# Two networks in one kernel: low halves, dots and one-hots placed anew

## The chip, the cores and the metric

The kernel runs on one core of a Trainium2 chip, in one launch. The metric is the device time in microseconds; a kernel's time is the median of its runs. The engines are named as the profile names them: PE is TensorE, DVE is VectorE, ACT is ScalarE, POOL is GpSimd, SP is SyncE (here only a queue that starts loads).

## The reference

The input is 256 tokens of width 1024, and two networks of two layers each follow one another. The first has three mixers and a feed-forward of inner width 2816: `x + (silu(h @ w_gate) * (h @ w_up)) @ w_down`. The second has attention over the tokens and a context of 256 more tokens, and a feed-forward made of experts, which is where most of the time goes:

```python
s1 = einsum('nhd,kd->nhk', q1, sub_keys[0]); s2 = einsum('nhd,kd->nhk', q2, sub_keys[1])
v1, i1 = top_k(s1, 16); v2, i2 = top_k(s2, 16)
top_s, pos = top_k(v1[..., :, None] + v2[..., None, :], 16)     # 16 of 16384 experts, 8 heads
expert = take_along_axis(i1 * 128 + i2, pos)
u = u_tab[expert]
act = gelu(einsum('nhkd,nd->nhk', u, hb))
out = einsum('nhk,nhkd->nd', softmax(top_s) * act, v_tab[expert])
```

Each of 256 tokens picks 128 of 16384 experts (rows of 1024 numbers in two tables, U and V), in each of two layers. In layer 0 the 256 context tokens pass through the experts too.

## The kernel before

Products need more than one pass of TensorE's fp32r format: an operand is split into a high half (`hi`, a copy by ACT) and a low half (`lo = x - hi`, a subtract), and a product is three matmuls, hi*hi, hi*lo and lo*hi. `Net.split` (lines 172 to 181) does this with ACT and, for `lo`, DVE or POOL.

**Experts for the main tokens, dense (`Dense`).** All 16384 experts are computed for all 256 tokens, as 128 groups of 128 experts, cut into parts: four of 32 groups in layer 0, two of 64 in layer 1. Three kinds of steps exist. A U step (`u_part`) loads 512 KB of U, splits it and makes 24 matmuls, then a gelu into the tile A. A one-hot step (`w_part`, called W here; 32 per part, 8 tokens each) builds on DVE a one-hot of the first index (`o1`), one of the second (`o2`), and two products with the gate (`og`); 16 matmuls turn these into the weights of the part's experts, and DVE multiplies A by them. A V step (`v_part`) loads 512 KB of V, splits it and a column of A (`w_hi`, `w_lo`) and makes 12 matmuls that add to the output. `mesh` interleaves such steps at a fixed ratio. The order in layer 0 before is: U0 (beside the routing); U1 with W0; V0 with W1; U2; V1 with W2; U3; V2 with W3; V3. In layer 1 it is U0; U1 with W0; V0 with W1; V1. The subtract of U goes to POOL and DVE by columns (`self.low`: POOL has 2 of 8 column blocks in parts 0 and 1 of layer 0, else 4 of 8), that of V half to each. Raw tiles, split tiles and one-hots have a few buffers each (3 and 1 more for raw tiles in layer 0), and the next load waits until the splits have read a raw tile.

**Experts for the context tokens, gathered (`peer_gather`).** POOL starts an indirect DMA for each of 256 U rows (128 tokens' row each, 512 KB) and 256 V rows. For a U row a dot with the token's vector follows: either POOL multiplies and ACT sums, or DVE does both in one instruction. The first block's first 60 rows (`EARLY`) use POOL, and of the rows from 118 on every third (`POOL_DOTS`). V rows go to TensorE in fours. These rows are started during the first network's layer 1, and run on through its feed-forward, the attention and the expert block of layer 0.

**The order of work.** The engines execute their queues in order. A scheduler puts the instructions into the queues by priority and by a simulated time; `rank` and `issue_after` set priorities of the gather and of the attention, which are issued among other work.

**The second feed-forward** (`First.ffn`, called for layer 1 in the scope `f1`) makes 22 blocks of `act` in one loop; a second loop loads `w_down` in 22 pieces, splits each (every fourth on POOL), splits `act` (its low half on POOL) and multiplies.

Of the kernel before, what the change touches and what calls it, by code (L numbers as in the profile page):

```python
# [297 lines left out]
class First:  # L298
# [209 lines left out]

    def ffn(self, l, x, after=None, more=None):

        nc, n, a = self.nc, self.n, self.a
        hT, _ = self.norm_T(x, self.vcol("ffn_norm_g", l, 8), "hT2")
        if after:
            after()
        act = self.zones["x"].tile([P, KF, S], F32, name="ffact")
        for c in range(KF):
            ps = self.psum("pgu")
            for i, name in enumerate(("ffn_w_gate", "ffn_w_up")):
                w = self.w.load(a[name][l, c], KD, P, "wgu")
                for k in range(KD):  # L520
                    n.mm3(ps[:, i * S : (i + 1) * S], part(w, k), part(hT, k), k == 0, k == KD - 1)
            th = self.t([P, S], "ffth")
            nc.scalar.activation(th, ps[:, :S], AF.Tanh, scale=0.5)
            nc.vector.tensor_scalar(th, th, 0.5, 0.5, op0=ALU.mult, op1=ALU.add)
            nc.vector.tensor_tensor(th, ps[:, :S], th, op=ALU.mult)
            nc.vector.tensor_tensor(act[:, c], ps[:, S:], th, op=ALU.mult)
        wd = a["ffn_w_down"][l].rearrange("(k p) c -> p k c", p=P)
        pss = [self.psum(f"pd{i}") for i in range(4)]
        for k in range(KF):
            ws = self.w if more is None or k % 2 else more  # L530
            if k % 4 < 2:
                w = part(ws.load(wd[:, k : k + 1], 1, D, "wd"), 0)
            else:
                if k % 2 == 0:
                    two = self.zones["x"].pair([P, 2, D], "wd2")
                w = part(two, k % 2)
                raw = ws.plain(wd[:, k : k + 1], 1, D, "wd")
                n.split(raw[:, 0], *w, eng2="gv"[k % 2])
            ak = self.z.pair([P, S], "ffak")
            n.split(act[:, k], *ak, eng2="g")  # L540
            for b in range(2):
                for hf in range(2):
                    n.mm3(pss[2 * b + hf], part(ak, slice(b * P, (b + 1) * P)), part(w, slice(hf * 512, (hf + 1) * 512)), k == 0, k == KF - 1)
        for b in range(2):
            for hf in range(2):
                xs = x[:, b, hf * 512 : (hf + 1) * 512]
                nc.vector.tensor_tensor(xs, pss[2 * b + hf], xs, op=ALU.add)
# [438 lines left out]
class Second:  # L986
# [408 lines left out]
    def peer_gather(self, slots, rows, out, gp, vp, act0, hm0):  # L1395
# [11 lines left out]
        def u_rows(b):  # L1407
# [4 lines left out]
            def dot(j, u):  # L1412
                o = act[:, j : j + 1]
                if j < EARLY if b == 0 and j < EARLY + GATHERS else j % POOL_DOTS == 0:
                    nc.gpsimd.tensor_tensor(u, u, hm, op=ALU.mult)  # L1415
                    nc.scalar.activation(u, u, AF.Copy, accum_out=o)
                else:
                    nc.vector.tensor_tensor_reduce(out=u, in0=u, in1=hm, scale=1.0, scalar=0.0, op0=ALU.mult, op1=ALU.add, accum_out=o)  # L1418
# [84 lines left out]
class Dense:  # L1503
# [9 lines left out]
    def __init__(self, net, ctx, x, h, l, col, parts, banks, raw):  # L1513
# [5 lines left out]
        self.parts = parts  # L1519
        self.low = ((2, 2, 4, 4), (4, 4))[l]  # L1520
        self.first = [sum(parts[:i]) for i in range(len(parts))]
# [32 lines left out]
    def u_part(self, f, A):  # L1554
# [3 lines left out]
        def split(i):  # L1558
# [3 lines left out]
            ul = self.pu.tile([P, KD, P], F32R, tag="lo", name="u_lo")  # L1562
            q = self.low[f]
            nc.scalar.activation(uh, u, AF.Copy)  # L1564
            for e, o, m in ((nc.gpsimd, 0, q), (nc.vector, q, KD)):
                if o < m:
                    e.tensor_tensor(ul[:, o:m], u[:, o:m], uh[:, o:m].bitcast(F32), op=ALU.subtract)  # L1567
            return uh, ul
# [69 lines left out]
    def v_part(self, f, W, starts, stops):  # L1638
# [4 lines left out]
        for i in range(H):  # L1643
# [4 lines left out]
            vl = self.pu.tile([P, D], F32R, tag="lo", name="v_lo")  # L1648
            nc.scalar.activation(vh, v, AF.Copy)  # L1649
            nc.gpsimd.tensor_tensor(vl[:, 0:512], v[:, 0:512], vh[:, 0:512].bitcast(F32), op=ALU.subtract)  # L1650
            nc.vector.tensor_tensor(vl[:, 512:], v[:, 512:], vh[:, 512:].bitcast(F32), op=ALU.subtract)  # L1651
            wh = self.po.tile([P, S], F32R, tag="wh", name="w_hi")
# [55 lines left out]
LOW = "gv"  # L1708
POOL_DOTS = 3
GATHER_CLASSES = ((32, 8), (512, 5), (1024, 2), (4096, 1))  # L1710
# [7 lines left out]
def build(tc, aps, out):  # L1718
    with ExitStack() as ctx:
# [99 lines left out]

        with f.scope("f1", FFN_ZONES, 6, {"w": 6}, "v", 4):  # L1820
            f.ffn(1, x, lambda: gather_on(GATHERS))
        fx.close()
        for l in range(L):
            last = l == L - 1
            with ExitStack() as cl:
# [70 lines left out]
                else:  # L1896
                    de.mesh((de.v_part(0, ab[0], True, False), parts[0]), (de.w_part(1, ab[1]), nw))
                    de.mesh((de.u_part(2, ab[0]), parts[2]))
                    de.mesh((de.v_part(1, ab[1], False, False), parts[1]), (de.w_part(2, ab[0]), nw))
                    de.mesh((de.u_part(3, ab[1]), parts[3]))  # L1900
                    de.mesh((de.v_part(2, ab[0], False, False), parts[2]), (de.w_part(3, ab[1]), nw))
# [51 lines left out]
```

## Time and profile before

| | |
|---|---|
| median of 3 runs | 3541.01 us (3537.23 to 3547.21) |
| profiled execution | 3555.65 us, span 3553.9 us |
| PE busy | 3114.9 us, 88% |
| DVE busy | 2635.4 us, 74% |
| POOL busy | 1920.3 us, 54% |
| ACT busy | 1426.0 us, 40% |
| HBM read | 753.44 MB |

The profile is of one execution; its times are from the span's start. Stages by what runs in them: the first network to 1115 us (its second feed-forward from 900); attention and scores of layer 0 to 1370; U0 with the routing to 1545; U1 with W0 to 1670; V0 with W1 and then U2 to 1985; V1 with W2 and then U3 to 2255; V2 with W3 and V3 to 2525; attention of layer 1 to 2735; its U0 to 2945, U1 with W0 to 3155, V0 with W1 to 3300, the rest of V to the end.

### The profile page before, as it was taken

What the parts mean: (1) busy time and instruction counts of PE and PEld (TensorE: products, weight loads), DVE (VectorE), ACT (ScalarE), POOL (GpSimd) and SP (SyncE); (2) the same over time, 40 slices, a digit from 0 to 9 for tenths busy, and PEclk for the clock granted to TensorE, in tenths of its full rate; (3) what the DMA queues carried; (4) which work ended last, traced back from release to release, by engine and by line L of the source; (5) the groups of instructions that cost most, each with busy time, mean ns of one, the idle gap of its engine ahead of it and who ended that gap; (6) DMA issues with size and microseconds to landing.
All of it is one profiled execution on the core that took longest, in us unless ns stands there. A gap on an engine that the chain in (4) does not pass through costs nothing. (4 is left out here: it accounts for less than half of the span.)

```text
span 3553.9 us, 58408 instructions
## 1 busy us (share of the span) xinstructions
PE 3114.9 (88%) x22044; PEld 2575.2 (72%) x22044; DVE 2635.4 (74%) x5055; ACT 1426.0 (40%) x2195; POOL 1920.3 (54%) x1368
## 2 busy tenths in 40 slices
PE   8979997688896768879878899999888899999999
PEld 6758895566795558867557658756668899986887
DVE  5647789774897789999875784675677826789777
ACT  4234543443543454433323333323454343443454
POOL 2113228656667576667557657666211465544665
PEclk9999999899898879989989999999899999999999
DMA  6555554667897567778768779878423454544555
GB/s 205 174 165 162 161 161 155 205 218 238 301 331 248 174 224 243 240 276 312 247 232 306 274 265 322 306 280 322 143 68 118 154 178 155 167 155 137 183 191 172
DMA packets 260970, 761.46 MB, mean 214 GB/s; under 512 B 26064, under 2 KB 81424, under 8 KB 260688
## 3 DMA queue, kind: packets, MB, share of 16 engines
q1 hardware_dynamic: 127856, 410.50, 34.5%
q0 software_dynamic: 79456, 289.18, 23.7%
q10 hardware_dynamic: 53376, 58.05, 5.0%
q8 instruction: 173, 2.83, 0.3%
q14 instruction: 109, 0.89, 0.1%
HBM read 753.44 MB, written 4.19 MB: 213 GB/s over the span
## 5 line engine op out<-in xcount | busy, mean ns | idle before, releaser
L1582 PE MATMUL aT<-h_hi,u_lo 128*128 128x256 f32 x2048 | 595.6, 292 | 53.6 <-POOL u_lo L1567 26.7
L1580 PE MATMUL aT<-h_hi,u_hi 128*128 128x256 f32 x2048 | 595.0, 291 | 7.5 <-ACT u_hi L1564 6.8
L1581 PE MATMUL aT<-h_lo,u_hi 128*128 128x256 f32 x2048 | 588.4, 288 | 0.0
L1650 POOL TENSOR_TENSOR v_lo<-v_raw,v_hi 128x512 fp32r<-128x512 f32 x256 | 398.7, 1564 | 247.3 <-ACT v_hi L1649 223.4
L1567 POOL TENSOR_TENSOR u_lo<-u_raw,u_hi 128x512 fp32r<-128x512 f32 (+1 forms) x256 | 362.7, 1425 | 293.0 <-ACT u_hi L1564 284.8
L1425 POOL DMA_INDIRECT ug<-in_peer_u,slot_e x256 | 311.8, 1218 | 285.5 <-DVE act L1418 122.2
L1649 ACT ACTIVATE v_hi<-v_raw 128x1024 fp32r<-128x1024 f32 x256 | 270.8, 1059 | 477.6 <-issue 222.0
L1564 ACT ACTIVATE u_hi<-u_raw 128x1024 fp32r<-128x1024 f32 x256 | 269.5, 1058 | 477.4 <-PE aT L1581 216.2
L1582 PEld LDWEIGHTS aT<-h_hi,u_lo 128*128 128x128 f32 x2048 | 400.8, 196 | 68.3 <-DVE u_lo L1567 30.5
L1580 PEld LDWEIGHTS aT<-h_hi,u_hi 128*128 128x128 f32 x2048 | 402.6, 197 | 14.7 <-ACT u_hi L1564 9.0
L1581 PEld LDWEIGHTS aT<-h_lo,u_hi 128*128 128x128 f32 x2048 | 402.4, 196 | 4.2 <-issue 4.2
L1664 PE MATMUL acc<-v_hi,w_lo 128*128 128x512 f32 x1024 | 339.2, 413 | 60.2 <-DVE w_lo L181 59.5
L1567 DVE TENSOR_TENSOR u_lo<-u_raw,u_hi 128x512 fp32r<-128x512 f32 (+1 forms) x256 | 262.5, 1027 | 163.1 <-ACT u_hi L1564 138.7
L1449 POOL DMA_INDIRECT vg<-in_peer_v,slot_eT x256 | 262.6, 1026 | 142.1 <-PE pv L1454 59.7
L1664 PE MATMUL acc<-v_lo,w_hi 128*128 128x512 f32 x1024 | 331.4, 405 | 0.1
L1664 PE MATMUL acc<-v_hi,w_hi 128*128 128x512 f32 x1024 | 308.6, 411 | 5.2 <-ACT w_hi L177 5.2
L1415 POOL TENSOR_TENSOR ug<-ug,hm 128x1024 f32<-128x1024 f32 x106 | 263.4, 2489 | 65.9 <-DMA ug<-in_peer_u,slot_e 62.3
L1651 DVE TENSOR_TENSOR v_lo<-v_raw,v_hi 128x512 fp32r<-128x512 f32 x256 | 203.5, 795 | 116.0 <-ACT v_hi L1649 102.9
L1664 PEld LDWEIGHTS acc<-v_hi,w_lo 128*128 128x128 f32 x1024 | 192.4, 195 | 119.6 <-DVE w_lo L181 74.7
L181 DVE TENSOR_TENSOR w_lo<-d_A,w_hi 128x256 fp32r<-128x256 f32 x256 | 264.0, 1033 | 3.7 <-ACT w_hi L177 3.5
L1418 DVE CUSTOM_DVE_ANT_0 ug<-ug,hm 128x1024 f32<-128x1024 f32 x150 | 212.3, 1423 | 37.9 <-DMA ug<-in_peer_u,slot_e 35.4
L1664 PEld LDWEIGHTS acc<-v_lo,w_hi 128*128 128x128 f32 x1024 | 199.2, 196 | 45.9 <-issue 2.0
(659 smaller groups left out, 7539.3 us busy)
## 6 DMA issues: line engine op xcount, KB each, us to landing
u_raw<-in_u_columns SPq DMA_DIRECT2D x256, 512.0 KB
v_raw<-in_peer_v SPq DMA_DIRECT2D x256, 512.0 KB
adaw<-in_ada_w ACTq DMA_DIRECT2D x96, 512.0 KB
wgu<-in_ffn_w_gate SPq DMA_DIRECT2D x44, 512.0 KB
wgu<-in_ffn_w_up SPq DMA_DIRECT2D x44, 512.0 KB
wd<-in_ffn_w_down SPq DMA_DIRECT2D x44, 512.0 KB
wpq<-in_peer_w_q SPq DMA_DIRECT2D x32, 512.0 KB
wqkv<-in_w_qkv SPq DMA_DIRECT2D x24, 512.0 KB
```

The lines of the kernel that those rows point to most:

```text
L181: e.tensor_tensor(lo, src, hi.bitcast(F32), op=ALU.subtract)
L1415: nc.gpsimd.tensor_tensor(u, u, hm, op=ALU.mult)
L1425: nc.gpsimd.indirect_dma_start(out=u, out_offset=None, in_=ut, in_offset=bass.IndirectOffsetOnAxis(ap=slots[b][0][:, j : j + 1], axis=0))
L1449: loads.append(nc.gpsimd.indirect_dma_start(out=four[q], out_offset=None, in_=vt, in_offset=bass.IndirectOffsetOnAxis(ap=slots[b][1][:, to ...
L1564: nc.scalar.activation(uh, u, AF.Copy)
L1567: e.tensor_tensor(ul[:, o:m], u[:, o:m], uh[:, o:m].bitcast(F32), op=ALU.subtract)
L1580: nc.tensor.matmul(o, uh[:, k], self.hh[:, k], start=k == 0, stop=False)
L1581: nc.tensor.matmul(o, uh[:, k], self.hl[:, k], start=False, stop=False)
L1582: nc.tensor.matmul(o, ul[:, k], self.hh[:, k], start=False, stop=k == KD - 1)
L1649: nc.scalar.activation(vh, v, AF.Copy)
L1650: nc.gpsimd.tensor_tensor(vl[:, 0:512], v[:, 0:512], vh[:, 0:512].bitcast(F32), op=ALU.subtract)
L1664: nc.tensor.matmul(self.acc[2 * b + hf], x[:, bs], y[:, hf * 512 : (hf + 1) * 512], start=s0, stop=s1)
```

## The change

In the expert blocks every low half of U and V is made by DVE as one subtract of 1024 columns. The dots of all gathered rows but the first 60 use DVE's one instruction. In layer 0 the one-hot steps W1 are interleaved with V0 and U2 together (64 steps instead of 32), and W2 with V1 and U3. The second feed-forward splits each block of `act` in the first loop, into two tiles that are kept (the new zone `y` of 22528 bytes a partition), and all low halves of its `w_down` that it splits itself go to DVE.

```diff
--- before.py
+++ after.py
@@ -506,13 +506,17 @@
                 xs = x[:, b, hf * 512 : (hf + 1) * 512]
                 nc.vector.tensor_tensor(xs, pss[hf][b], xs, op=ALU.add)
 
-    def ffn(self, l, x, after=None, more=None):
+    def ffn(self, l, x, after=None, more=None, early=False):
+
 
         nc, n, a = self.nc, self.n, self.a
         hT, _ = self.norm_T(x, self.vcol("ffn_norm_g", l, 8), "hT2")
         if after:
             after()
-        act = self.zones["x"].tile([P, KF, S], F32, name="ffact")
+        if early:
+            act = self.zones["x"].tile([P, KF, S], F32R, name="ffact_hi"), self.zones["y"].tile([P, KF, S], F32R, name="ffact_lo")
+        else:
+            act = self.zones["x"].tile([P, KF, S], F32, name="ffact")
         for c in range(KF):
             ps = self.psum("pgu")
             for i, name in enumerate(("ffn_w_gate", "ffn_w_up")):
@@ -523,7 +527,11 @@
             nc.scalar.activation(th, ps[:, :S], AF.Tanh, scale=0.5)
             nc.vector.tensor_scalar(th, th, 0.5, 0.5, op0=ALU.mult, op1=ALU.add)
             nc.vector.tensor_tensor(th, ps[:, :S], th, op=ALU.mult)
-            nc.vector.tensor_tensor(act[:, c], ps[:, S:], th, op=ALU.mult)
+            if early:
+                nc.vector.tensor_tensor(th, ps[:, S:], th, op=ALU.mult)
+                n.split(th, *part(act, c))
+            else:
+                nc.vector.tensor_tensor(act[:, c], ps[:, S:], th, op=ALU.mult)
         wd = a["ffn_w_down"][l].rearrange("(k p) c -> p k c", p=P)
         pss = [self.psum(f"pd{i}") for i in range(4)]
         for k in range(KF):
@@ -535,9 +543,12 @@
                     two = self.zones["x"].pair([P, 2, D], "wd2")
                 w = part(two, k % 2)
                 raw = ws.plain(wd[:, k : k + 1], 1, D, "wd")
-                n.split(raw[:, 0], *w, eng2="gv"[k % 2])
-            ak = self.z.pair([P, S], "ffak")
-            n.split(act[:, k], *ak, eng2="g")
+                n.split(raw[:, 0], *w, eng2="v" if early else "gv"[k % 2])
+            if early:
+                ak = part(act, k)
+            else:
+                ak = self.z.pair([P, S], "ffak")
+                n.split(act[:, k], *ak, eng2="g")
             for b in range(2):
                 for hf in range(2):
                     n.mm3(pss[2 * b + hf], part(ak, slice(b * P, (b + 1) * P)), part(w, slice(hf * 512, (hf + 1) * 512)), k == 0, k == KF - 1)
@@ -1411,7 +1422,7 @@
 
             def dot(j, u):
                 o = act[:, j : j + 1]
-                if j < EARLY if b == 0 and j < EARLY + GATHERS else j % POOL_DOTS == 0:
+                if b == 0 and j < EARLY:
                     nc.gpsimd.tensor_tensor(u, u, hm, op=ALU.mult)
                     nc.scalar.activation(u, u, AF.Copy, accum_out=o)
                 else:
@@ -1517,7 +1528,6 @@
         self.hh, self.hl = h
         self.pw, self.pr = None, raw
         self.parts = parts
-        self.low = ((2, 2, 4, 4), (4, 4))[l]
         self.first = [sum(parts[:i]) for i in range(len(parts))]
         self.pa = ctx.enter_context(tc.tile_pool(name=f"d_a{l}", bufs=1, reuse_waits="tile"))
         self.i = 0
@@ -1560,11 +1570,7 @@
             nc.sync.dma_start(u, cols[self.first[f] + i])
             uh = self.pu.tile([P, KD, P], F32R, tag="hi", name="u_hi")
             ul = self.pu.tile([P, KD, P], F32R, tag="lo", name="u_lo")
-            q = self.low[f]
-            nc.scalar.activation(uh, u, AF.Copy)
-            for e, o, m in ((nc.gpsimd, 0, q), (nc.vector, q, KD)):
-                if o < m:
-                    e.tensor_tensor(ul[:, o:m], u[:, o:m], uh[:, o:m].bitcast(F32), op=ALU.subtract)
+            self.split(u, uh, ul)
             return uh, ul
 
         ahead = [split(0)]
@@ -1646,9 +1652,7 @@
             nc.sync.dma_start(v, vv[:, i2])
             vh = self.pu.tile([P, D], F32R, tag="hi", name="v_hi")
             vl = self.pu.tile([P, D], F32R, tag="lo", name="v_lo")
-            nc.scalar.activation(vh, v, AF.Copy)
-            nc.gpsimd.tensor_tensor(vl[:, 0:512], v[:, 0:512], vh[:, 0:512].bitcast(F32), op=ALU.subtract)
-            nc.vector.tensor_tensor(vl[:, 512:], v[:, 512:], vh[:, 512:].bitcast(F32), op=ALU.subtract)
+            self.split(v, vh, vl)
             wh = self.po.tile([P, S], F32R, tag="wh", name="w_hi")
             wl = self.po.tile([P, S], F32R, tag="wl", name="w_lo")
             self.split(W[:, i], wh, wl)
@@ -1706,7 +1710,6 @@
 MORE = 56
 UFIRST = EARLY + GATHERS + MORE - P
 LOW = "gv"
-POOL_DOTS = 3
 GATHER_CLASSES = ((32, 8), (512, 5), (1024, 2), (4096, 1))
 ATTN_CLASSES = (
     ((32, 24), (256, 8), (1024, 8), (2048, 4), (4096, 3), (8192, 4)),
@@ -1817,8 +1820,8 @@
                     pass
                 at[0] = tc.cur_priority
 
-        with f.scope("f1", FFN_ZONES, 6, {"w": 6}, "v", 4):
-            f.ffn(1, x, lambda: gather_on(GATHERS))
+        with f.scope("f1", dict(FFN_ZONES, y=((22528, 1),)), 6, {"w": 6}, "v", 4):
+            f.ffn(1, x, lambda: gather_on(GATHERS), early=True)
         fx.close()
         for l in range(L):
             last = l == L - 1
@@ -1894,10 +1897,9 @@
                     de.mesh((de.v_part(0, ab[0], True, False), parts[0]), (de.w_part(1, ab[1]), nw))
                     de.mesh((de.v_part(1, ab[1], False, True), parts[1]))
                 else:
-                    de.mesh((de.v_part(0, ab[0], True, False), parts[0]), (de.w_part(1, ab[1]), nw))
-                    de.mesh((de.u_part(2, ab[0]), parts[2]))
-                    de.mesh((de.v_part(1, ab[1], False, False), parts[1]), (de.w_part(2, ab[0]), nw))
-                    de.mesh((de.u_part(3, ab[1]), parts[3]))
+                    for i in range(2):
+                        vu = itertools.chain(de.v_part(i, ab[i], i == 0, False), de.u_part(i + 2, ab[i]))
+                        de.mesh((vu, parts[i] + parts[i + 2]), (de.w_part(i + 1, ab[1 - i]), nw))
                     de.mesh((de.v_part(2, ab[0], False, False), parts[2]), (de.w_part(3, ab[1]), nw))
                     de.mesh((de.v_part(3, ab[1], False, True), parts[3]))
                 de.finish(out if last else None)
```

## Rows read from the trace of the kernel before

**Rows 1.** Windows: length, busy PE, PEld, DVE, ACT, POOL (instructions), PEclk, DMA share, GB/s.

```profile
1370.00:1545.00 175.00, 131.26 (x977) 124.86 (x975) 170.96 (x502) 71.60 (x94) 111.05 (x85) 0.90 0.67 225
...
1545.00:2525.00 980.00, 875.52 (x6865) 658.76 (x6865) 702.89 (x1159) 318.71 (x444) 650.51 (x544) 0.94 0.81 284
...
1670.00:1985.00 315.00, 259.58 (x1951) 199.30 (x1950) 226.99 (x334) 97.43 (x136) 204.50 (x169) 0.90 0.78 267
3155.00:3300.00 145.00, 133.43 (x945) 99.22 (x945) 140.76 (x226) 50.60 (x75) 58.77 (x38) 0.95 0.42 139
```

**Rows 2.** TensorE's waits, 1545 to 2525 us: us in total, times, longest.

```profile
PE acc L1664 <- DVE w_lo L181: 52.1, 27, 5.6
PE gps L1630 <- DVE og L1626: 26.3, 8, 7.3
PE aT L1582 <- POOL u_lo L1567: 16.7, 7, 3.4
PE aT L1582 <- DVE u_lo L1567: 2.7, 2, 2.0
```

**Rows 3.** Timeline, 1841 to 1850 us: start, length, instruction, idle before it.

```profile
1841.07 0.62 PE L1664 MATMUL acc<-v_hi,w_lo 128*128 128x512 f32 x2
...
1842.00 5.32 DVE L1621 TENSOR_TENSOR o<-iota,d_iT 128x1024 f16<-128x1024 bf16 x1
...
1843.22 2.33 POOL L1415 TENSOR_TENSOR ug<-ug,hm 128x1024 f32<-128x1024 f32 x1
...
1848.72 0.80 PE L1664 MATMUL acc<-v_hi,w_lo 128*128 128x512 f32 x1 [5.60 <-DVE w_lo L181]
...
1849.74 1.05 PE L1664 MATMUL acc<-v_lo,w_hi 128*128 128x512 f32 x2
```

**Rows 4.** DVE groups by shape, 1670 to 2525 us: busy us, mean ns, idle before.

```profile
L1621 DVE TENSOR_TENSOR o<-iota,d_iT 128x1024 f16<-128x1024 bf16 x97 | 112.5, 1160 | 0.0
L1651 DVE TENSOR_TENSOR v_lo<-v_raw,v_hi 128x512 fp32r<-128x512 f32 x128 | 110.9, 867 | 60.0 <-ACT v_hi L1649 46.9 <-issue 11.9 <-PE acc L1664 0.9
L181 DVE TENSOR_TENSOR w_lo<-d_A,w_hi 128x256 fp32r<-128x256 f32 x128 | 105.3, 825 | 3.7 <-ACT w_hi L177 3.5
L1567 DVE TENSOR_TENSOR u_lo<-u_raw,u_hi 128x512 fp32r<-128x512 f32 x64 | 92.1, 1445 | 79.1 <-ACT u_hi L1564 54.8 <-issue 19.2 <-PE aT L1582 3.1
```

**Rows 5.** Single lines, whole span: count, ns min/median/max, first and last start (L1415 from 1115 us).

```profile
L181 DVE TENSOR_TENSOR w_lo<-d_A,w_hi x256: 404/668/6835, 1684.4 to 3541.2; 128x256 fp32r<-128x256 f32 x128
L181 DVE TENSOR_TENSOR wqkv_lo<-wqkv,wqkv_hi x36: 1207/1222/1228, 228.3 to 2587.0; 128x1024 fp32r<-128x1024 f32 x36
...
L1651 DVE TENSOR_TENSOR v_lo<-v_raw,v_hi x256: 676/692/3481, 1676.2 to 3540.6; 128x512 fp32r<-128x512 f32 x128
...
L1621 DVE TENSOR_TENSOR o<-iota,d_iT x192: 673/681/5575, 1547.6 to 3290.6; 128x1024 f16<-128x1024 bf16 x192
...
L1449 POOL DMA_INDIRECT vg<-in_peer_v,slot_eT x256: 937/942/2162, 1385.9 to 2487.2; - x128
...
L1415 POOL TENSOR_TENSOR ug<-ug,hm x46: 2330/2392/3426, 1226.0 to 2032.8; 128x1024 f32<-128x1024 f32 x46
```

**Rows 6.** DVE groups by shape, 1115 to 1545 us.

```profile
L1418 DVE CUSTOM_DVE_ANT_0 ug<-ug,hm 128x1024 f32<-128x1024 f32 x74 | 103.1, 1397 | 35.7 <-DMA ug<-in_peer_u,slot_e 35.4 <-DMA hm<-d_crows 0.3
L1567 DVE TENSOR_TENSOR u_lo<-u_raw,u_hi 128x768 fp32r<-128x768 f32 x37 | 44.3, 1196 | 0.0
```

**Rows 7.** The window with the highest DMA rate in the expert block.

```profile
2200.00:2250.00 50.00, 50.00 (x413) 42.15 (x413) 23.34 (x20) 18.24 (x21) 36.82 (x32) 1.00 0.95 336
```

**Rows 8.** TensorE's waits in layer 1's expert block, 2735 to 3300 us.

```profile
PE aT L1582 <- DVE u_lo L1567: 11.2, 7, 3.2
PE acc L1664 <- DVE w_lo L181: 7.4, 8, 1.4
PE aT L1582 <- POOL u_lo L1567: 6.0, 4, 2.8
```

**Rows 9.** TensorE's waits in the second feed-forward, 900 to 1115 us.

```profile
PE pd L190 <- POOL wd_lo L181: 3.1, 1, 3.1
```

## The prediction

> **What bounds the kernel now.** I read the windows by stage first, then TensorE's waits, then one stall in the timeline, then the DVE groups and the spread of single lines, and last the DMA rate.
>
> The windows show that the change lands in two places. In layer 0's expert block, 1545 to 2525 us, TensorE is busy 876 of 980 us at a mean granted clock of 0.94 and the DMA engines run at 284 GB/s [rows 1]. Its worst part is the stretch in which V of part 0 runs beside the one-hots of part 1 and U of part 2 follows: 260 of 315 us busy, clock 0.90 [rows 1]. So TensorE is the engine that the end waits for, and it is neither full nor at full clock. In layer 1 it is nearly full; only 3155 to 3300 us, where V meets the one-hots, has DVE at 141 of 145 us [rows 1].
>
> The waits of TensorE in layer 0's block name who is late: `w_lo` 52.1 us, `og` 26.3, the GpSimd half of `u_lo` 16.7, the DVE half 2.7, together 97.8 us [rows 2]. Three are DVE work, yet DVE is busy only 703 of 980 us there [rows 1]. So not DVE's total is the limit but single late instructions.
>
> One stall shows why. At 1842.00 the one-hot compare of 128x1024, which takes 0.68 us at the median [rows 5], takes 5.32 us; GpSimd runs a 2.33 us multiply (and two `u_lo` halves around it) meanwhile, and TensorE then waits 5.60 us for the `w_lo` queued behind it. A pair of matmuls took 0.62 us before and 1.05 us after: TensorE came back at or near the lower of its two levels, 1.2 GHz [rows 3]. A GpSimd elementwise instruction thus costs DVE its whole length, and TensorE the wait plus a slow stretch after it. The Trainium skill states this ("SBUF — State Buffer", section "Who interferes with whom"): DVE with two SBUF inputs and a GpSimd instruction that reads SBUF lock each other out whole.
>
> The DVE groups say how much: from 1670 to 2525 us `o` means 1.160 us against 0.681 at its median, `w_lo` 0.825 against a minimum of 0.404, `v_lo` 0.867 against 0.692, and the 512-wide `u_lo` 1.445 against the same 0.69 [rows 4, 5]. That is 97 x 0.48 + 128 x 0.42 + 128 x 0.175 + 64 x 0.755 = 171 us of DVE time lost to the lock.
>
> **The change, part by part.**
>
> *Low halves on DVE alone.* One 1024-wide subtract costs 1.22 us (the median of `wqkv_lo`) against 0.69 for the half [rows 5], so DVE gets 0.53 us more on each of 128 V and 64 U steps after 1670: +102 us. GpSimd's halves go, and with them a second engine that SP's next load has to wait for before a raw tile is free.
>
> *Dots on DVE.* The 46 multiplies of 2.39 us leave GpSimd, with their 46 ScalarE sums; they lie between 1226 and 2033 us [rows 5]. On DVE each costs 1.40 us [rows 6]. At an even pace 21 fall after 1670: +29 us. A row's tile is free for the next gather only when its dot is done, so GpSimd's next gather now waits on DVE alone; behind it in GpSimd's queue stand, through the attention, the first step of the root and some rotary products, which DVE and then TensorE wait for. Before, two rows in three had that wait already, and the third a longer one (2.39 us and the sum), so I add nothing. The first 60 dots stay on GpSimd. The DVE balance of the expert block is thus -171 + 102 + 29 = -40 us, if what is left on GpSimd locks nothing. What is left is the row gathers, 0.942 us each at the median and 2.162 at most [rows 5]: mostly undisturbed. By the skill's rule (same page and section) descriptor generation needs only the write side, so a `tensor_tensor` would not meet it at all and the whole 171 us would go; by the row's maximum a small part stays. I take the saving as incomplete.
>
> *One-hots over V and U.* W1 and W2 issue 32 steps each of 4 DVE compares and products, 16 matmuls and one DVE multiply. Half of each is moved past the 32 U steps that follow (their copies, subtracts, 768 matmuls, gelus), no DMA is moved, and SP's order of loads stays. With 0.40 us, the free `w_lo`, as an estimate for each of the four narrow instructions of a one-hot step (all 256 wide as well), DVE work per V step falls from 4.5 us (`v_lo` 0.87 + `w_lo` 0.83 + `o` 1.16 + 1.6) to 2.8 (1.22 + 0.40 + half of 0.68 + 1.6). Its price: the last one-hot step now ends together with U instead of 32 steps earlier, and the next V step needs it, so TensorE waits through multiply, `w_hi` and `w_lo` (256 wide, 0.4 us each by the same estimate, and the handing over between engines) at two seams: 2 us each, +4 us.
>
> Together: of the 97.8 us of waits I take 60 per cent as gone, 59 us, because some are TensorE's own head-of-line waits that any order leaves; of the clock's loss, (1 - 0.94) x 980 = 59 us, a quarter, 15 us, since seams and DMA gaps lower it too. That is -74 us, and with the seams -70. The bounds: nothing, if DVE's added 131 us eat what the lock gives back; -150, if all 157 us go. The transfers cap it: 980 us at 284 GB/s, done at the 336 GB/s that the fullest 50 us show [rows 7], take 828 us, so -152.
>
> *Layer 1.* The waits are 11.2 (DVE `u_lo`), 7.4 (`w_lo`) and 6.0 (GpSimd `u_lo`) [rows 8], and the clock of 0.95 over 145 us costs 7 [rows 1]; 32 us, of which I take 18. `u_lo` beside the routing is DVE queueing that a longer subtract keeps. Bounds 0 and -28. After 3300 us nothing can be won: TensorE is full.
>
> *The second feed-forward.* Its splits leave GpSimd: 22 `ffak_lo` go to DVE early in the gate/up loop, 5 `wd_lo` too. The wait that shows is 3.1 us on `wd_lo` [rows 9]; DVE takes the 22 small subtracts (0.40 each, 9 us, by the like-sized `w_lo`) below TensorE's matmuls of that loop. I take -4, bounds -10 and +5: the new 22 KB zone may hold back loads of the next block that now lie where it will be, which would show as a late first projection.
>
> *Attention and first U part, 1115 to 1545.* 25 dots at 1.40 us put +35 us on DVE, and 37 `u_lo` grow from 768 to 1024 columns, 1.196 us contended [rows 6] to about 1.22 free: nothing. Between 1370 and 1545 DVE is busy 171 of 175 us [rows 1], so this cover is thin. Against it 25 x 2.39 = 60 us of locking multiplies go. I take 0, bounds -20 and +35; here alone DVE is the limit.
>
> Sum: -70 - 18 - 4 + 0 = -92 us. Against the profiled execution's own 3555.65 us that is 3463.7; the median of the runs shown lies 14.6 us lower, so 3449 us.
>
> **Rivals.**
>
> *Transfers or gather bind* (chance 0.2). Gathers that no longer queue behind GpSimd arithmetic run earlier and take bandwidth from U and V loads; later the dense steps alone can't fill it. For it: the mean is already 284 of 336 GB/s. Against: gather matmuls have fixed places in TensorE's queue, so gathers can't run far ahead. If the block's mean only rises to 300 GB/s, it takes 980 x 284/300 = 928 us, -52; with dense loads starved for half of that, -26, and about -10 from elsewhere: 3541 - 36 = 3505 us. The skill ("SBUF — State Buffer", section "A bandwidth-pool intuition that's wrong") puts the ceiling of HBM at about 358 GB/s; by it the block could not go under an estimated 777 us. No run here shows that rate.
>
> *DVE becomes the limit* (0.09; slower). The place is 1115 to 1545 and the routing of both layers: +35 us of dots and +0.5 us on each half of `u_lo`, with gathers still disturbing DVE. If the lock gives nothing back there, the price is the 35 us in layer 0 and, for as many U steps as its 37 there, 37 x 0.53 = 20 us in layer 1's routing, 55; with 15 won later, 3581 us. It decides if `o`, dots and subtracts keep their present means beside gathers alone. Against it: gathers at 0.942 us median.
>
> *The relief is hidden* (0.11). The scheduler orders instructions by its own durations; if it knew nothing of the lock, its new order may put new waits where old ones went. Then about 3537 us, within 0.3 per cent.
>
> **How the numbers follow.** The forecast has 0.60: 3385 to 3495 us by itself (-156, most of both bounds, to -46). The 80 per cent range leaves out the slower rival and a little on each end: 3385 to 3535. A difference of 0.3 per cent, 11 us, is about what a measurement of this kernel can tell. Faster takes the forecast, the transfer rival and a part of the hidden one: 0.60 + 0.20 + 0.05 = 0.85; same 0.06; slower 0.09.
>
> **What will show it.** Right: `w_lo` near 0.41 us, `o` near 0.68, `v_lo` and `u_lo` at 1.22 throughout the expert blocks; TensorE's waits on `w_lo` and `og` under 40 us between the start of layer 0's one-hots and the end of its V; its clock there at 0.96 or more; the stretch 980 us shorter by about 70; V after the one-hots of layer 1 unchanged. Wrong: means that stay long although GpSimd only gathers; DVE at 95 per cent through attention with late routing; a DMA rate above 320 GB/s with TensorE waiting on raw tiles; waits of several us at the seams from U to V.

## The result and the profile after

The changed kernel takes 3431.24 us (median of 4 runs, 3417.58 to 3435.1) against 3541.18 (4 runs, 3537.23 to 3547.21): ratio 0.9681, with a 95% interval of 0.9651 to 0.9711. Forecast were 3449 us and a range of 3385 to 3535. The profiled execution spans 3429.0 us against 3553.9. The difference of 125 us splits into four stretches, cut at the start of the same instructions in both traces (the last add of the second feed-forward, the first one-hot, the last add of layer 0, the last add of layer 1); what follows the last add, some 1 us of the difference, is left out:

| stretch, us | before | after | difference | forecast |
|---|---|---|---|---|
| start to end of the second feed-forward | 1137 | 1139 | +2 | -4 |
| attention and first U part of layer 0 | 410 | 447 | +37 | 0 |
| expert block of layer 0, from its first one-hot | 977 | 834 | -143 | -70 |
| layer 1 | 1024 | 1004 | -20 | -18 |

The windows by stage of the kernel after (columns as in [rows 1]):

```profile
1139.00:1586.00 447.00, 291.90 (x1747) 248.40 (x1747) 380.64 (x975) 149.02 (x219) 190.59 (x155) 0.82 0.72 242
1586.00:2421.00 835.00, 823.80 (x6865) 632.89 (x6865) 560.24 (x1132) 301.12 (x411) 298.26 (x278) 0.99 0.88 315
3046.00:3158.00 112.00, 108.88 (x874) 83.68 (x873) 109.44 (x206) 43.98 (x64) 0.00 (x0) 1.00 0.45 147
```

The middle row answers to the row of 980 us in [rows 1]: the same 6865 matmul records now lie in 835 us. TensorE's idle time fell from 104 to 11 us, and its busy time from 876 to 824 at a granted clock of 0.99 instead of 0.94. In the last row DVE is still busy in 109 of 112 us, as it was in 141 of 145, where V meets the one-hots of layer 1.

TensorE's waits in the expert block of layer 0 after, all that the view lists (against [rows 2]):

```profile
PE gps L1636 <- DVE og L1632: 5.4, 1, 5.4
PE pv L1465 <- issue: 1.9, 2, 1.2
PE acc L1668 <- ACT w_hi L177: 1.0, 1, 1.0
PE pv L1465 <- DMA vg<-in_peer_v,slot_eT: 0.2, 1, 0.2
```

97.8 us on DVE's and GpSimd's products have become 5.4, one wait at the very first one-hot. The matmuls of the gathered V rows (`pv`) wait for 2.1 us here; the view of the kernel before lists no wait of theirs. DVE's groups between 1600 and 2430 us after, by shape (against [rows 4]):

```profile
L181 DVE TENSOR_TENSOR v_lo<-v_raw,v_hi 128x1024 fp32r<-128x1024 f32 x128 | 156.9, 1225 | 87.9 <-ACT v_hi L177 85.8 <-issue 1.7
L181 DVE TENSOR_TENSOR u_lo<-u_raw,u_hi 128x1024 fp32r<-128x1024 f32 x91 | 111.2, 1222 | 79.2 <-ACT u_hi L177 79.2
L1627 DVE TENSOR_TENSOR o<-iota,d_iT 128x1024 f16<-128x1024 bf16 x125 | 85.6, 685 | 0.0
L1632 DVE TENSOR_TENSOR og<-o,d_gT 128x256 f16<-128x256 f16 x250 | 61.4, 286 | 0.0
L1638 DVE SCALAR_TENSOR_TENSOR d_A<-gps,d_A 128x256 f32<-128x256 f32 x127 | 53.5, 421 | 77.6 <-PE gps L1636 77.0
L181 DVE TENSOR_TENSOR w_lo<-d_A,w_hi 128x256 fp32r<-128x256 f32 x128 | 53.3, 418 | 2.4 <-ACT w_hi L177 2.4
```

Two groups of the kernel before that [rows 4] doesn't show, 1548 to 2525 us:

```profile
L1626 DVE TENSOR_TENSOR og<-o,d_gT 128x256 f16<-128x256 f16 x256 | 97.4, 418 | 0.0
...
L1632 DVE SCALAR_TENSOR_TENSOR d_A<-gps,d_A 128x256 f32<-128x256 f32 x128 | 53.3, 417 | 68.9 <-PE gps L1630 47.7 <-remote 17.8 <-PE acc L1664 3.3
```

The product `og`, with two inputs in SBUF, fell from 0.418 to 0.286 us. The multiply of A (`d_A`), which reads the matmuls' result `gps` and only one tile of SBUF, took 0.417 us before (0.427 at most) and 0.421 after: GpSimd's work never lengthened it.

And the spread of single lines after, over the whole span (against [rows 5]):

```profile
L181 DVE TENSOR_TENSOR w_lo<-d_A,w_hi x256: 408/418/426, 1717.0 to 3418.1; 128x256 fp32r<-128x256 f32 x128
...
L1627 DVE TENSOR_TENSOR o<-iota,d_iT x192: 670/682/755, 1586.1 to 3158.3; 128x1024 f16<-128x1024 bf16 x192
```

The longest `w_lo` takes 0.426 us where it took 6.835, and the longest `o` 0.755 where it took 5.575 [rows 5]; a stall like the one of [rows 3] is not there any more. TensorE's waits in layer 1's expert block after (2615 to 3158 us, against [rows 8]):

```profile
PE aT L1588 <- DVE u_lo L181: 11.2, 24, 2.0
PE aT L1586 <- ACT u_hi L177: 6.0, 6, 1.9
PE acc L1668 <- DVE w_lo L181: 1.5, 9, 0.2
```

The waits on `w_lo` and on GpSimd's `u_lo` went; those on DVE's `u_lo` beside the routing stayed at 11.2 us.

The 37 us that were lost lie ahead of the first one-hot. The gathers and dots there (1139 to 1586 us after):

```profile
L1436 POOL DMA_INDIRECT ug<-in_peer_u,slot_e x125 | 160.4, 1283 | 230.2 <-DVE act L1429 117.5 <-DVE i L1322 17.0 <-DVE v L1324 16.2
L1429 DVE CUSTOM_DVE_ANT_0 ug<-ug,hm 128x1024 f32<-128x1024 f32 x124 | 151.2, 1223 | 49.4 <-DMA ug<-in_peer_u,slot_e 49.4
```

The same groups before, in the same stretch (1137 to 1548 us):

```profile
L1425 POOL DMA_INDIRECT ug<-in_peer_u,slot_e x95 | 121.2, 1276 | 92.7 <-DVE act L1418 45.0 <-issue 10.3 <-DVE i L1311 10.1
L1418 DVE CUSTOM_DVE_ANT_0 ug<-ug,hm 128x1024 f32<-128x1024 f32 x68 | 93.2, 1373 | 26.8 <-DMA ug<-in_peer_u,slot_e 26.4 <-DMA hm<-d_crows 0.3
L1415 POOL TENSOR_TENSOR ug<-ug,hm 128x1024 f32<-128x1024 f32 x28 | 72.6, 2594 | 26.2 <-DMA ug<-in_peer_u,slot_e 23.3 <-DMA hm<-d_crows 2.6
```

Before, 68 + 28 = 96 dots stand ahead of the first one-hot; after, 124. So DVE does 56 dots more there: the 28 that GpSimd did, and 28 that stood in the block. They add 151.2 - 93.2 = 58 us, but DVE's busy time in the stretch grows by only 17 us (364 to 381), because other instructions got shorter (the low halves `wpq_lo` the most, 31.8 to 19.3). The other 20 of the 37 us are idle time of DVE (47 to 66 us). The rows above show it: DVE waits 49.4 us for gathered rows in place of 26.8, where before GpSimd waited 26.2 us for the rows of its own dots. TensorE's wait for the routing (its transpose, on `go`) grew from 6.8 to 27.9 us, the longest there after.

### The profile page after: what moved, and what is told of

Same layout as the page of the kernel before. It is cut to its first block, busy times and chain, and to the rows that moved or that the text cites. A ratio compares the mean times of both kernels' runs of the same rounds, so it can differ in the third digit from the quotient of the medians.

```text
span 3429.0 us, 56877 instructions
## 1 busy us (share of the span) xinstructions
PE 3063.0 (89%) x22044; PEld 2548.2 (74%) x22044; DVE 2457.0 (72%) x5174; ACT 1377.3 (40%) x2103; POOL 1017.1 (30%) x783
## 4 chain that ended last, share of the span: by engine, by line
PE 61%; DVE 19%; DMA 8%; issue 8%; POOL 3%; ACT 2%; SPq 0%; POOLq 0%; DVEq 0%; ACTq 0%
PE acc L1668 19%; PE aT L1586 5%; PE aT L1588 5%; PE aT L1587 5%; PE pv L1465 3%; DMA ug<-in_peer_u,slot_e 3%; DMA adaw<-in_ada_w 2%; PE gps L1636 2%; DVE u_lo L181 2%; DVE ug L1429 2%; PE sps L189 2%; PE sps L190 1%; PE sps L191 1%; POOL ug L1436 1%; PE ada L1060 1%
## 5 line engine op out<-in xcount | busy, mean ns | idle before, releaser
L181 DVE TENSOR_TENSOR v_lo<-v_raw,v_hi 128x1024 fp32r<-128x1024 f32 x256 | 313.6, 1225 | 198.9 <-ACT v_hi L177 195.8
L181 DVE TENSOR_TENSOR u_lo<-u_raw,u_hi 128x1024 fp32r<-128x1024 f32 x256 | 312.2, 1220 | 179.6 <-ACT u_hi L177 179.5
L1460 POOL DMA_INDIRECT vg<-in_peer_v,slot_eT x256 | 276.5, 1080 | 382.8 <-PE pv L1465 306.6
L1668 PE MATMUL acc<-v_lo,w_hi 128*128 128x512 f32 x1024 | 316.7, 391 | 0.0
L1668 PE MATMUL acc<-v_hi,w_hi 128*128 128x512 f32 x1024 | 284.4, 397 | 1.0 <-ACT w_hi L177 1.0
L1429 DVE CUSTOM_DVE_ANT_0 ug<-ug,hm 128x1024 f32<-128x1024 f32 x196 | 240.5, 1231 | 60.2 <-DMA ug<-in_peer_u,slot_e 59.9
L1668 PEld LDWEIGHTS acc<-v_hi,w_hi 128*128 128x128 f32 x1024 | 186.4, 188 | 43.6 <-issue 5.9
L191 PE MATMUL pgu<-hT_hi,wgu_lo 128*128 128x256 f32 x704 | 201.6, 287 | 7.7 <-DVE wgu_lo L181 6.2
L189 PE MATMUL pgu<-hT_hi,wgu_hi 128*128 128x256 f32 x704 | 200.2, 285 | 0.9 <-ACT wgu_hi L177 0.9
L190 PE MATMUL pgu<-hT_lo,wgu_hi 128*128 128x256 f32 x704 | 199.6, 284 | 0.0
```

Of the source, the lines that this page charges most:

```text
L181: e.tensor_tensor(lo, src, hi.bitcast(F32), op=ALU.subtract)
L189: mm(out, a[0], b[0], start=start, stop=False)
L190: mm(out, a[0], b[1], start=False, stop=False)
L191: mm(out, a[1], b[0], start=False, stop=stop)
L1460: loads.append(nc.gpsimd.indirect_dma_start(out=four[q], out_offset=None, in_=vt, in_offset=bass.IndirectOffsetOnAxis(ap=slots[b][1][:, to ...
L1668: nc.tensor.matmul(self.acc[2 * b + hf], x[:, bs], y[:, hf * 512 : (hf + 1) * 512], start=s0, stop=s1)
```

## The experiments

Two theories. *Lock*: GpSimd's elementwise instructions, by what they read, hold up DVE, and their removal is the gain. *Crowding*: DVE simply has too much to do in each V step that shares its time with a one-hot step, and spreading the one-hots over V and U is what relieves it. Stage times below are from one profile each; ratios are against the kernel before on the same chip (medians there 3556.46 us for the first four rows, 3558.51 for the next four and 3558.62 for the last four). idle_reads and idle_writes ran once each. "Dots" counts those between the end of the second feed-forward and the first one-hot.

| kernel | us | ratio, 95% | attention + U | dots | block 0 | layer 1 |
|---|---|---|---|---|---|---|
| splits_only | 3439.37 | 0.9678, 0.9662 to 0.9694 | 422 | 100 | 865 | 1005 |
| mesh_only | 3545.51 | 0.9976, 0.9960 to 0.9991 | 415 | 96 | 961 | 1018 |
| dots_only | 3526.40 | 0.9911, 0.9894 to 0.9927 | 439 | 121 | 917 | 1019 |
| no_mesh | 3430.12 | 0.9651, 0.9635 to 0.9667 | 445 | 124 | 842 | 1004 |
| idle_reads | 3512.73 | one run | 446 | 124 | 898 | 1029 |
| idle_writes | 3463.20 | one run | 447 | 124 | 879 | 1007 |
| attn_pool_dots | 3427.65 | 0.9629, 0.9584 to 0.9674 | 427 | 106 | 859 | 1007 |
| pool_until_block | 3421.14 | 0.9622, 0.9582 to 0.9662 | 425 | 103 | 857 | 1007 |
| after_again | 3432.82 | 0.9647, 0.9626 to 0.9667 | 448 | 124 | 845 | 1006 |
| no_early | 3444.41 | 0.9674, 0.9653 to 0.9695 | 439 | 124 | 851 | 1004 |
| pool_until_block_2 | 3424.48 | 0.9627, 0.9607 to 0.9646 | 423 | 103 | 864 | 1007 |
| pool_until_block_no_mesh | 3409.95 | 0.9581, 0.9555 to 0.9608 | 423 | 103 | 841 | 1009 |

**One part at a time (the kernel before, with one edit).** The low halves alone:

```diff
-            ...
-            for e, o, m in ((nc.gpsimd, 0, q), (nc.vector, q, KD)):
-                ...
+            self.split(u, uh, ul)
...
-            nc.gpsimd.tensor_tensor(vl[:, 0:512], ...)
-            nc.vector.tensor_tensor(vl[:, 512:], ...)
+            self.split(v, vh, vl)
```

> Kernel before, with the low halves of U and V on DVE alone (dots, one-hots, feed-forward as before). The block is layer 0 from its first one-hot step to its last add: 977 us before, 834 after. Lock theory (GpSimd arithmetic blocks DVE, and TensorE waits for the late instruction): the block falls to about 890, the whole by about 85, w_lo near 0.5 us, since only the remaining multiplies still block. Crowding theory (too much DVE work beside each V step, which the one-hots over V and U relieve): DVE has more to do per V step, the block stays at 960 to 1000 and the whole within 20 of before.

Measured: nearly the whole gain, 117 us, more than the lock theory expected; the block falls to 865 us and `w_lo` to 0.418. The block of this kernel, by the windows:

```profile
1559.00:2424.00 865.00, 833.06 (x6865) 635.30 (x6865) 592.10 (x1150) 319.27 (x444) 398.82 (x321) 0.99 0.89 319
```

The one-hots over V and U alone:

```diff
+                    for i in range(2):
+                        vu = itertools.chain(de.v_part(i, ab[i], i == 0, False), de.u_part(i + 2, ab[i]))
+                        de.mesh((vu, parts[i] + parts[i + 2]), (de.w_part(i + 1, ab[1 - i]), nw))
```

> Kernel before, with the one-hots W1 and W2 over V and U steps alone (all arithmetic placed as before). Lock theory: blocked instructions stay, block 977 to about 955, the whole about -20. Crowding theory: block to about 890, the whole about -85.

Measured: 0.24% faster, 16 us in the block, most of its disturbance still there: `o` means 1.34 us between 1600 and 2510 us of its trace, and TensorE waits 28.9 us on `og` and 27.8 on `w_lo` in the block. Beside these stand 18.1 us of waits on `d_A` that the kernel before doesn't have.

The dots alone:

```diff
-                if j < EARLY if b == 0 and j < EARLY + GATHERS else j % POOL_DOTS == 0:
+                if b == 0 and j < EARLY:
```

> Kernel before, with the dots of all gathered rows but the first 60 on DVE alone. Both theories: attention and the first U part of layer 0 (1139 to 1586 us after, 1137 to 1548 before) grow by about 30 to 40, because DVE is the limit there. Lock theory: the block loses 13 to 21 multiplies of 2.4 us and falls by about 25, the whole +10. Crowding theory: the block grows by as many dots, about 20, the whole +55.

Measured: 0.89% faster, a sign that both theories missed. It costs 29 us ahead of the one-hots and gives 60 back in the block.

The changed kernel with the old order of V, U and one-hots (the four lines that the diff removes are back):

```diff
-                    for i in range(2):
-                        vu = itertools.chain(...)
-                        ...
+                    de.mesh((de.v_part(0, ab[0], True, False), parts[0]), (de.w_part(1, ab[1]), nw))
+                    de.mesh((de.u_part(2, ab[0]), parts[2]))
+                    ...
```

> Kernel after, with the one-hots W1 and W2 put back beside V alone. Lock theory: block 834 to about 860, the whole 3431 to about 3455. Crowding theory: block to about 915, the whole about 3510.

Measured: 0.9651, the same as the changed kernel's 0.9647 (after_again), and a block of 842 us against 834 and 845 in two profiles of the changed kernel; the lock theory, too, had expected a loss, of about 25 us. V of part 0 beside the one-hots W1 in this kernel:

```profile
1707.00:1835.00 128.00, 127.61 (x1060) 84.70 (x1061) 104.03 (x246) 44.06 (x65) 54.79 (x48) 0.99 0.89 316
```

and in the kernel before:

```profile
1683.00:1851.00 168.00, 134.67 (x987) 91.05 (x988) 137.80 (x250) 47.16 (x71) 98.23 (x82) 0.89 0.73 241
```

With the old order and a quiet GpSimd, TensorE is full and DVE is busy for 104 of 128 us; before, it took DVE 138 us to do as many instructions. There was no crowding to relieve; this theory falls.

**The lock by itself (the changed kernel, with GpSimd work that nobody reads).** In each V step two subtracts that read SBUF, or one tiny subtract and four memsets that only write:

```diff
             self.split(v, vh, vl)
+            idle = self.pa.tile([P, 384], F32, tag="idle", name="idle")
+            for j in range(2):
+                vf = vl[:, j * 384 : (j + 1) * 384].bitcast(F32)
+                nc.gpsimd.tensor_tensor(idle, vf, vf, op=ALU.subtract)
```

```diff
             self.split(v, vh, vl)
+            idle = self.pa.tile([P, 384], F32, tag="idle", name="idle")
+            vf = vl[:, 0:8].bitcast(F32)
+            nc.gpsimd.tensor_tensor(idle[:, 0:8], vf, vf, op=ALU.subtract)
+            for j in range(4):
+                nc.gpsimd.memset(idle, 0.0)
```

> Kernel after, with two GpSimd subtracts of 384 columns added behind every V split (256 V steps); they read v_lo, write a scratch tile that nobody reads, and hold up no tile that TensorE has not still to read itself. DVE has no work more. Lock theory: DVE instructions beside them take up to 0.9 us longer, w_lo means 0.7 to 1.0 us in place of 0.42 in the V steps, TensorE waits on DVE again in the block (20 to 60 us in place of none), and the whole is 20 to 60 us over after. If GpSimd cost DVE time before only as the maker of half of v_lo and u_lo, w_lo stays at 0.42 and the whole within 10 of after.

> Kernel after, with four GpSimd memsets of 384 columns added behind every V split, tied to it by a subtract of 8 columns. By a lock that only a GpSimd instruction reading memory takes, w_lo and v_lo stay at 0.42 and 1.22 us and the whole within 10 us of after. If any GpSimd work holds DVE, w_lo grows as with the subtracts.

DVE's groups of idle_reads, 1600 to 2430 us:

```profile
L181 DVE TENSOR_TENSOR v_lo<-v_raw,v_hi 128x1024 fp32r<-128x1024 f32 x114 | 159.0, 1395 | 45.0 <-ACT v_hi L177 30.2 <-POOL idle L1659 12.6 <-issue 1.6
...
L1627 DVE TENSOR_TENSOR o<-iota,d_iT 128x1024 f16<-128x1024 bf16 x123 | 99.4, 808 | 0.0
...
L181 DVE TENSOR_TENSOR w_lo<-d_A,w_hi 128x256 fp32r<-128x256 f32 x112 | 73.1, 655 | 0.0
```

and of idle_writes:

```profile
L181 DVE TENSOR_TENSOR v_lo<-v_raw,v_hi 128x1024 fp32r<-128x1024 f32 x124 | 151.5, 1222 | 91.2 <-ACT v_hi L177 73.0 <-POOL idle L1658 10.0 <-PE acc L1673 3.4
...
L1627 DVE TENSOR_TENSOR o<-iota,d_iT 128x1024 f16<-128x1024 bf16 x120 | 81.9, 682 | 0.0
...
L181 DVE TENSOR_TENSOR w_lo<-d_A,w_hi 128x256 fp32r<-128x256 f32 x122 | 50.8, 418 | 0.0
```

GpSimd's added work in the same stretch, in idle_reads and then in idle_writes:

```profile
L1659 POOL TENSOR_TENSOR idle<-v_lo 128x384 f32<-128x384 f32 x226 | 243.3, 1077 | 66.6 <-DVE v_lo L181 49.8 <-DVE xv L1481 2.2 <-DVE xr_y L220 1.3
```

```profile
L1660 POOL MEMSET idle<- 128x384 f32 x492 | 207.0, 421 | 26.6
L1658 POOL TENSOR_TENSOR idle<-v_lo 128x8 f32<-128x8 f32 x123 | 39.6, 322 | 43.4 <-DVE v_lo L181 35.7 <-DVE xv L1481 1.2
```

Reading instructions lengthen `w_lo` from 0.418 to 0.655 us and `o` from 0.685 to 0.808; memsets leave both as they were. So it is the reads. Layer 1 has no gathers and shows this alone: its V part takes 401 us with reads and 379 with memsets, as with neither. The sizes were missed: idle_reads is 81 us over the changed kernel, where 20 to 60 was expected, though TensorE's waits on DVE in the block (10.9 us on `w_lo`, beside the one at the first one-hot) stay below the 20 to 60. The memsets cost layer 0's block 34 to 45 us (against 845 and 834) and the whole 32, which no theory had expected (within 10 us was). The waits of TensorE in idle_writes, 1600 to 2500 us:

```profile
PE pv L1465 <- issue: 14.3, 9, 2.4
PE pv L1465 <- DMA vg<-in_peer_v,slot_eT: 13.5, 8, 3.5
```

The matmuls of the gathered V rows come late. The gathers now stand in GpSimd's queue behind the memsets and behind the subtract, which itself waits 35.7 us for `v_lo`; how much each adds is not told apart. idle_reads has the same two waits at 14.9 and 9.5 us, with 10.9 on `w_lo` beside them. The kernel before has no such waits, so TensorE's waits for late gathers are no part of what the change gave back in the block.

**The 37 us ahead of the one-hots.** In the changed kernel, every third dot of the attention back on GpSimd:

```diff
-                if b == 0 and j < EARLY:
+                if (j < EARLY or j >= EARLY + GATHERS and j % 3 == 0) if b == 0 else j < UFIRST and j % 3 == 0:
```

> Kernel after, with every third dot of the rows that are gathered before the expert block (rows 118 on of the first 128 and the first 46 of the second) back on GpSimd and ScalarE, as in the kernel before; the rest of the dots stays on DVE. If the dots cost DVE time where it is the limit, attention and the first U part of layer 0 go from 447 us to about 420, the block stays at about 835, the whole is 3405. If what they cost there is made up by rows that are then done before the block, the block grows by as much and the whole stays at 3431.

and, beside that, a quarter of the low halves of U part 0 in layer 0 too:

```diff
-            self.split(u, uh, ul)
+            if self.l == 0 and f == 0:
+                nc.scalar.activation(uh, u, AF.Copy)
+                for e, o, m in ((nc.gpsimd, 0, 2), (nc.vector, 2, KD)):
+                    e.tensor_tensor(ul[:, o:m], u[:, o:m], uh[:, o:m].bitcast(F32), op=ALU.subtract)
+            else:
+                self.split(u, uh, ul)
```

> As attn_pool_dots, and the first U part of layer 0 keeps GpSimd's 256 of 1024 columns of u_lo. If DVE's load beside the routing is the limit there, another 7 us go from the first U part (159 to 152 in the two kernels that differ so) and the whole is about 3395; if the lock outweighs it, attn_pool_dots is the faster.

Measured: 20 us less ahead of the one-hots in the one and 22 in the other, and 25 and 22 more in the block (14 and 12, against the 845 of after_again); the ratios' intervals overlap that of the changed kernel. The stage follows the dots that stand ahead of the first one-hot: 410 to 422 us at 96 to 100 dots, 423 to 427 at 103 to 106, 439 to 448 at 121 to 124. But GpSimd does 28 to 30 of the dots in the first group, 19 in the second and none in the third, so these kernels don't tell the count of dots from the engine that does them. And a dot that is not done there is done in the block.

**The rest.** The changed kernel again, and with the second feed-forward of the kernel before (`early` off, its zone `y` gone):

```diff
-            f.ffn(1, x, lambda: gather_on(GATHERS), early=True)
+            f.ffn(1, x, lambda: gather_on(GATHERS))
```

> The changed kernel unaltered, beside the three that follow on one chip: ratio to before 0.968, as measured.

> Kernel after, with the second feed-forward as in the kernel before (its low halves split late and in part on GpSimd). From the end of the first feed-forward to that of the second the kernels with the early split take 493 to 503 us, those without 503 to 516. If the early split is worth what GpSimd's low halves cost there, this stretch is 10 us longer and the whole 10 us over after_again; if it is only the order of the schedule, the whole is within 5 us.

Measured: 3432.82 and 3444.41 us; the intervals overlap, so by the whole time early splitting is worth about 12 us, not surely more than nothing. The traces are clearer, if the feed-forward is cut out of the stretch that was expected about, which has the mixers in it too: from its first matmul to its last add it takes 198 us with the early split and 214 without. In the nine profiles with the early split it takes 196 to 199 us, in the five without 211 to 216. The gain lies in its second loop, over `w_down`. This loop in the kernel before and after:

```profile
1053.00:1138.00 85.00, 66.69 (x264) 52.59 (x264) 67.05 (x71) 29.42 (x50) 70.78 (x49) 0.88 0.76 260
```

```profile
1075.50:1139.50 64.00, 60.05 (x266) 49.39 (x264) 53.95 (x79) 22.70 (x31) 25.98 (x22) 1.00 0.80 289
```

The kernel pool_until_block once more, and the same with the old order of V, U and one-hots (the edit of no_mesh on top):

> pool_until_block again, for a comparison with the changed kernel on one chip. If its 10 us are real: 10 us under after_again, ratio to before about 0.965; if they are noise between chips, equal.

> pool_until_block, with the one-hots W1 and W2 beside V alone as in the kernel before. By the lock theory the interleaving gives next to nothing once GpSimd is quiet: within 8 us of pool_until_block_2. By the crowding theory it is 20 us or more slower, since the block of pool_until_block still has waits on DVE.

Measured: 3424.48 and 3409.95 us. The first is 8 us under after_again with overlapping intervals. The second beats the changed kernel too: 0.9581 (0.9555 to 0.9608) lies wholly under its 0.9626 to 0.9667. That the old order is 14.5 us faster here fits neither theory, and why it is stays open. Its block of layer 0:

```profile
1554.00:2395.00 841.00, 828.11 (x6865) 630.57 (x6865) 577.64 (x1172) 298.92 (x408) 331.16 (x298) 0.99 0.90 325
```

## Why the prediction was right, and where it was not

**The bound and the lock: right.** `w_lo` at 0.418, `o` at 0.685, `v_lo` and `u_lo` at 1.22 us are the signs it named, and DVE instructions beside gathers alone run undisturbed (the longest `o` takes 0.755 us). The pair idle_reads and idle_writes shows the cause: near-equal GpSimd time (586 and 561 us in the block), and only instructions that read lengthen DVE's. This is what the Trainium skill states ("SBUF — State Buffer", section "Who interferes with whom"): a GpSimd instruction that reads SBUF contends with a DVE instruction of two SBUF inputs, one that only writes doesn't. The runs agree, and so does `d_A`, which has one input in SBUF and kept its 0.42 us.

**The block's term was mis-sized: -143, forecast -70.** It took 59 of 97.8 us of waits and a quarter of the clock's loss. TensorE's idle time fell by 104 - 11 = 93 us, and its busy time by 876 - 824 = 52, of which it had taken 15. "TensorE's own head-of-line waits that any order leaves" were not there: 8.5 us of waits are left in all, the longest 5.4. And the clock came back with the waits gone: the granted clock is 1.00, the higher of its two levels, in every 50 us between 1600 and 2400 us, where in the kernel before it lay between 0.86 and 1.00. The upper bound of 150 was the better estimate. The DVE balance behind the term was too high as well: -40 us forecast, -140 measured (700 to 560 us busy from the first one-hot on). It counted 29 us of dots into the block, where dots fell from 49 to 29 us because the order pulled them forward, and it left out what the lock cost `og` and the narrow one-hot, 52 us.

**"One-hots over V and U": wrong.** The step credited it with DVE work per V step of 4.5 to 2.8 us and seams of +4. Without it, with GpSimd quiet, the block takes 842 us and the kernel the same time; in the best version it costs, 3424.48 against 3409.95 us, though these intervals (0.9607 to 0.9646, 0.9555 to 0.9608) still touch. That DVE was late did not mean that it had too much work: what it had too much of was lock. No wait shows at the two seams.

**"Dots on DVE" and the attention: +37, forecast 0 with a bound of +35.** The prediction weighed 25 dots against 60 us of locking multiplies and saw that the cover is thin. It left out that an order worked out anew also pulls dots forward: beside the 28 that left GpSimd, 28 more stand ahead of the first one-hot. And where it wrote "so I add nothing" for the wait between gather and dot, DVE now waits itself for the rows of all dots, 49.4 us in place of 26.8, with the rest of its work queued behind. The lock's relief is there (the same dot takes 1.223 instead of 1.373 us) but is the smaller. That these two make up the 37 us is read from the traces; neither was tried by itself. In sum, once the low halves are off GpSimd, the dots on DVE are worth about nothing: -31 and -23 us in the block (splits_only's 865 to the 834 and 842 of the changed kernel and no_mesh), +26 and +23 ahead of it (422 to 447 and 445).

**Layer 1: right (-20, forecast -18).** 16 of the 20 us lie in its V part (395 to 379). The waits on DVE's `u_lo` stayed at 11.2 us, as foreseen.

**The second feed-forward was mis-sized: -16, forecast -4 with a bound of -10.** From its first matmul to its last add it went from 212 to 197 us. The forecast priced the one wait of 3.1 us on `wd_lo`; the loop over `w_down` got back all of its waits (9.0 us) and its clock (0.88 to 1.00), and fell from 85 to 64 us, while the loop before it grew by 6. The first row of the table hides this because the feed-forward starts 17 us later in the profile after (942 against 925 us). The change leaves the code before it as it was, and in the other kernels it starts between 922 and 939 us; why so late here is not explained.

**The rivals.** Transfers did not bind: the block's rate rose from 284 to 315 GB/s, and TensorE waits 0.2 us for the landing of gathered rows. The stretch ahead of the one-hots grew as the rival of DVE as the limit said, by two thirds of its price, but without its sign (DVE is busy 85% of it, not 95), and the block paid four times as much back. The relief was not hidden by new waits in the block.

The forecast came out 18 us too long (33 by the profiled executions, 3463.7 against 3430.73), because the missing 73 us in the block and the 37 on the other side partly cancel, as do the 12 us missing in the feed-forward and the 17 of its late start. That the total fits better than its parts is luck.

## What to carry to other kernels

When single instructions of DVE run far over their own minimum while GpSimd works, take from GpSimd what reads SBUF before spreading DVE's work, even if DVE's nominal load grows: here, of three edits to the expert blocks, the subtracts alone brought nearly all of the gain. If TensorE's granted clock is low where waits of one cause stand, count both as gone with the cause, not a part of each: here the clock went from 0.94 to 0.99 with the waits. A stretch where DVE is nearly full should be costed by what the new order puts there, not only by what the edit names, and by the waits that move to DVE with the work.

## What the runs showed of the hardware beside this

GpSimd's elementwise work has a second price, its queue: 128 steps with 4 memsets of 0.42 us and a small subtract that waits for `v_lo`, none of which lengthens a DVE instruction, made the gathers late and the block 34 to 45 us longer, in one run.

A DMA rate stood above the ceiling that the prediction quoted. The window of the kernel after soon after the one-hots begin:

```profile
1600.00:1650.00 50.00, 48.85 (x549) 42.32 (x548) 43.85 (x100) 15.77 (x19) 27.77 (x27) 1.00 0.99 380
```

380 GB/s over 50 us is more than the 358 of the Trainium skill ("SBUF — State Buffer", section "A bandwidth-pool intuition that's wrong"), which the page works out as a stack's rate divided by two cores, while this kernel runs on one; the measurement decides, and the 777 us worked out from the page's figure is not shown to be a floor for the block.
